# Windowed attention: the softmax sums applied after the value product instead of to the probabilities

## The chip, the cores and the metric

The kernel runs on one core of a Trainium2 chip. The metric is the time of one execution on the device in microseconds (us), given as the median of several runs. A core has five engines with an instruction queue each: TensorE (PE in the profile, with PEld for its weight loads), VectorE (DVE), ScalarE (ACT), GpSimd (POOL) and SyncE (SP, which here only starts DMA transfers). Each queue runs in order. An engine waits at an instruction until the semaphores that it names have been raised by the engines or transfers it depends on, and everything behind that instruction waits with it.

## The reference: what is computed

One layer of a hybrid encoder on 1024 tokens of width 1024, all in float32. Two mixers read the same normalised input: a windowed attention (8 heads of 64, two groups of keys and values, each query block of 128 tokens sees its own block and the two beside it) and a two-directional gated delta rule (4 heads of 128). Their outputs are multiplied with an output matrix and added to the input; a feed-forward part with squared ReLU and a last norm follow. The change touches the attention alone:

```python
scores = einsum("bnqkgd,bnskd->bnkgqs", qb, kb) * 64 ** -0.5
scores = scores + bias                                  # by head and distance
scores = where(valid, scores, -1e30)
probs = softmax(concatenate([scores, sink_col], -1), -1)[..., :-1]
out = einsum("bnkgqs,bnskd->bnqkgd", probs, vb)
```

The sink is one more logit of each head. It takes part in the maximum and in the sum, and has no value row.

## The kernel before

Tokens lie in 8 chunks of 128. The attention is a stream of 16 steps, one for each chunk `n` and key group `kv`; a step handles four heads, one for each `g`. In `attn_scores` the PE makes the scores of a head in one PSUM bank (a high and a low part of the keys, lines 542 and 543), and one DVE instruction (line 544) adds the bias, writes the scores to SBUF and keeps each row's maximum in `mx`. The DVE turns the four maxima into the negated maximum `nm` with the sink in it (line 551), and makes the sink's exponent `es` (line 552). The ACT takes the exponentials in place and keeps their row sums in `sm` (lines 553 and 556). The DVE adds the sink's part and inverts the sums (lines 557 and 558), and the four score tiles are multiplied with the inverse sums (line 561: three heads on DVE, the fourth on POOL). `attn_transpose` turns the normalised probabilities on the PE, one bank for each key block (line 571), and the ACT copies each bank to SBUF (line 573). After the second group of a chunk, `attn_value` multiplies them with the values: six float32 products of 512 columns for a chunk with three key blocks, four at the two ends (line 583), into one bank. Each row of that bank is a value channel and each column a query of a head, so a query's factor lies along the columns there. The DVE copies the bank out (line 586), and a transfer takes it to DRAM for the output projection.

The attention is one of two streams that `weave` merges by weights when the program is written. The other inverts triangular blocks (`invert`, lines 718 to 762) and then runs the delta rule in two directions (`scan`): 8 steps each way, in which small products (line 795) and DVE operations (lines 808 to 841) follow each other. Later in that stream `load_wout` brings in and splits the output matrix (ACT line 861, DVE and POOL line 863). After the attention, the output projection of the attention part (`out_attn`) and of the delta rule's part (`out_all`) run beside the rest of the scan. The program is written under a scheduler which reorders the instructions of each engine within their dependencies, so the order in which they stand is not that of the source alone; it is fixed when the kernel is built.

Tiles come from rings: `psA` and `psB` are four PSUM banks each, `pt` is a ring of 12 SBUF tiles, `nm` a ring of 12 small ones (128x4) for the maxima and sums of a step. The attention uses `psA` for scores, transposes and values; scan and inversion use `psB`.

Of the kernel before, what the change touches and what calls it, by code (L numbers as in the profile page):

```python
# [12 lines left out]
AF = mybir.ActivationFunctionType  # L13
ALU = mybir.AluOpType
AX = mybir.AxisListType

P = 128
# [60 lines left out]
class Block:  # L78
# [448 lines left out]
                self.nc.sync.dma_start(out=t[32 * m:32 * m + 32], in_=src)  # L527
            self.bias.append(t)

    def attn_scores(self, n, kv, mx, q, mk):  # L530
        nc = self.nc
        lo, hi = max(n - 1, 0), min(n + 2, NT)
        width, boff = (hi - lo) * P, (lo - (n - 1)) * P
        tiles = []
        for gp in range(2):
            s = mk((P, 2, 3 * P))
            for i in range(2):
                g = 2 * gp + i
                head = 4 * kv + g
                ps = self.ps("psA")  # L540
                keys = slice(lo * P, hi * P)
                nc.tensor.matmul(ps[:, :width], q[:, g, :], self.kh[kv][:, keys], start=True, stop=False)
                nc.tensor.matmul(ps[:, :width], q[:, g, :], self.kl[kv][:, keys], start=False, stop=True)
                nc.vector.tensor_tensor_reduce(out=s[:, i, :width], in0=ps[:, :width],
                                               in1=self.bias[head // 2][:, head % 2, boff:boff + width],
                                               op0=ALU.add, op1=ALU.max, scale=1.0, scalar=-3e38,
                                               accum_out=mx[:, g:g + 1])
            tiles.append(s)
        nm, es, sm = (self.small((P, 4), tag="nm", bufs=12) for _ in range(3))
        ns = self.nsink[:, 4 * kv:4 * kv + 4]  # L550
        nc.vector.scalar_tensor_tensor(out=nm, in0=mx, scalar=-1.0, in1=ns, op0=ALU.mult, op1=ALU.min)
        nc.vector.tensor_tensor(out=es, in0=nm, in1=ns, op=ALU.subtract)
        nc.scalar.activation(out=es, in_=es, func=AF.Exp)
        for g in range(4):
            s = tiles[g // 2][:, g % 2, :width]
            nc.scalar.activation(out=s, in_=s, func=AF.Exp, bias=nm[:, g:g + 1], accum_out=sm[:, g:g + 1])
        nc.vector.tensor_tensor(out=sm, in0=sm, in1=es, op=ALU.add)
        nc.vector.reciprocal(out=sm, in_=sm)
        for g in range(4):
            s = tiles[g // 2][:, g % 2, :width]  # L560
            (nc.gpsimd if g == 3 else nc.vector).tensor_scalar(out=s, in0=s, scalar1=sm[:, g:g + 1], scalar2=None,
                                                               op0=ALU.mult)
        return tiles, list(range(lo, hi))

    def attn_transpose(self, tiles, kbs):
        nc = self.nc
# [7 lines left out]
            out.append(pt)  # L574
        return out

    def attn_value(self, n, pts, kbs):
        nc = self.nc
        ps = self.ps("psA")
        last = len(kbs) - 1  # L580
        for j in range(last, -1, -1):
            for kv in (1, 0):
                nc.tensor.matmul(ps[64 * kv:64 * kv + 64, :], self.va[:, kbs[j], 64 * kv:64 * kv + 64],
                                 pts[kv][j].rearrange("p g q -> p (g q)"), start=j == last, stop=j == 0)
        o = self.pt()
        nc.vector.tensor_copy(out=o, in_=ps)
        nc.sync.dma_start(out=self.mad[n], in_=o)

    def query(self, n, kv):
# [5 lines left out]
    def attention(self):  # L595

        steps = [(n, kv) for n in range(NT) for kv in range(2)]
        qs = self.qs
        open_, pts = [], []

        def close():
            n, kv, tiles, kbs = open_.pop(0)
            pts.append(self.attn_transpose(tiles, kbs))
            yield 1.3
            if kv == 1:
                self.attn_value(n, pts[:], kbs)
                pts.clear()
                yield 2.6

        for i, (n, kv) in enumerate(steps):  # L610
            mk = self.pg if i % 3 == 2 else self.wr
            open_.append((n, kv, *self.attn_scores(n, kv, self.small((P, 4), tag="nm", bufs=12), qs.pop(0), mk)))
            if i + 2 < len(steps):
                qs.append(self.query(*steps[i + 2]))
            yield 1.3
            if len(open_) > 2:
                yield from close()
        while open_:
            yield from close()
# [758 lines left out]
```

## Time and profile before

| | |
|---|---|
| three runs | 1249.07, 1250.0 and 1251.16 us, median 1250.0 |
| the profiled execution | 1248.56 us, of which the span from first to last instruction is 1246.8 |
| PE busy | 1184.7 us, 95% of the span |
| DVE, ACT, POOL busy | 854.8, 620.7 and 577.9 us |
| first and last score product of the attention (line 543) | start at 333.4 and 447.3 us |
| last value product (line 583) | starts at 462.0 us |

The profile is one execution, seen by the hardware profiler. Its views are: the page with busy times and groups of instructions; the timeline, instructions in order of time; the waits, which say who waited for whom; and tables of busy time by stretch, in which PEclk is the clock that the PE was granted (1.00 is full). The records of PE products have modelled ends and overlap, so the time that one product costs in a row of products is read from the distance of their starts and not from the duration of a record. Names such as psA<-ident,wr stand for the tile that is written and, behind the arrow, for what is read. A float32 product appears as two PE records, a transpose as one.

### The profile page before, as it was taken

To read this page: it belongs to the slowest core of one execution; us is meant where nothing else is said; L and a number is where in the kernel's file an instruction comes from. 1 tells how busy PE (TensorE), PEld (TensorE's weight loads), DVE (VectorE), ACT (ScalarE), POOL (GpSimd) and SP (SyncE) were. 2 spreads that over 40 slices of the span, in tenths; PEclk is the share of its full clock that TensorE was granted. 3 is DMA by queue.
4 is the path that set the end of the run, shared out by engine and by line. 5 is a ranking of instruction groups with operands and counts; after the bars stand their busy time and mean duration, and the time that the engine had idled before them with its cause. 6 is when DMAs were issued, how large, how long until landed. Compare 5 with 4: busy or idle time off the path is not lost. (4 is left out here: it accounts for less than half of the span.)

```text
span 1246.8 us, 18527 instructions
## 1 busy us (share of the span) xinstructions
PE 1184.7 (95%) x6482; PEld 968.6 (78%) x6482; DVE 854.8 (69%) x1528; ACT 620.7 (50%) x1347; POOL 577.9 (46%) x488
## 2 busy tenths in 40 slices
PE   7999999899789989998899999999999999999997
PEld 5788877778568868877788888888777888888885
DVE  5677667982389986676645453544669797886976
ACT  6455688345485752125464554545545433444343
POOL 5354211352432333244564535535455555655595
PEclk9999999899889999999999999999999999999999
DMA  6134444341855668122234444443688624444333
GB/s 240 52 121 137 114 157 148 132 127 43 228 169 156 185 219 296 60 85 86 84 120 158 145 153 144 150 165 134 226 284 282 230 85 158 152 125 146 98 89 135
DMA packets 121630, 187.62 MB, mean 150 GB/s; under 512 B 11043, under 2 KB 64416, under 8 KB 121537
## 3 DMA queue, kind: packets, MB, share of 16 engines
q1 hardware_dynamic: 96708, 152.58, 37.6%
q10 hardware_dynamic: 16381, 29.67, 6.2%
q0 software_dynamic: 8448, 4.20, 1.8%
q8 instruction: 51, 0.84, 0.3%
q14 instruction: 42, 0.34, 0.1%
HBM read 122.39 MB, written 63.49 MB: 149 GB/s over the span
## 5 line engine op out<-in xcount | busy, mean ns | idle before, releaser
L124 PE MATMUL psA<-pg,wh 128*128 128x512 f32 x416 | 166.4, 401 | 2.1 <-ACT pt L456 2.1
L126 PE MATMUL psA<-pg,wl 128*128 128x512 f32 x416 | 165.7, 398 | 0.0
L125 PE MATMUL psA<-pg,wh 128*128 128x512 f32 x416 | 165.3, 397 | 0.0
L120 POOL TENSOR_TENSOR wl<-wr,wh 128x512 fp32r<-128x512 f32 x44 | 69.4, 1600 | 153.0 <-ACT wh L119 152.9
L1152 DVE TENSOR_TENSOR pg<-pg 128x512 fp32r<-128x512 f32 x112 | 123.1, 1133 | 19.5 <-ACT pg L1151 19.5
L120 POOL TENSOR_TENSOR wh<-wr,wh 128x512 fp32r<-128x512 f32 x32 | 47.7, 1511 | 129.1 <-ACT wh L119 129.1
L125 PE MATMUL psA<-pg,pg 128*128 128x512 f32 x256 | 99.8, 391 | 0.4 <-POOL pg L120 0.4
L124 PE MATMUL psA<-pg,pg 128*128 128x512 f32 x256 | 99.0, 391 | 1.1 <-DVE pg L1197 0.9
L126 PE MATMUL psA<-pg,pg 128*128 128x512 f32 x256 | 99.7, 389 | 0.0
L1069 ACT ACTIVATE pt<-pt 128x512 f32<-128x512 f32 x64 | 40.4, 631 | 117.6 <-DVE pt L1059 117.6
L120 POOL TENSOR_TENSOR pg<-wr,pg 128x512 fp32r<-128x512 f32 x48 | 73.4, 1558 | 50.8 <-ACT pg L119 50.8
L124 PEld LDWEIGHTS psA<-pg,wh 128*128 128x128 f32 x416 | 79.5, 191 | 19.9 <-ACT pt L456 2.4
L125 PEld LDWEIGHTS psA<-pg,wh 128*128 128x128 f32 x416 | 79.4, 191 | 18.4 <-issue 0.9
L126 PEld LDWEIGHTS psA<-pg,wl 128*128 128x128 f32 x416 | 79.4, 191 | 16.9
L1151 ACT CAST pg<-pg 128x512 fp32r<-128x512 f32 x112 | 66.8, 620 | 42.0 <-DMA pg<-sd 30.3
L125 PE MATMUL psB<-pg,pg 128*128 128x512 f32 x192 | 75.0, 391 | 0.8 <-POOL pg L120 0.7
L126 PE MATMUL psB<-pg,pg 128*128 128x512 f32 x192 | 75.0, 390 | 0.3 <-DVE pg L1152 0.3
L124 PE MATMUL psB<-pg,pg 128*128 128x512 f32 x192 | 74.7, 390 | 0.3 <-ACT pg L1151 0.3
L119 ACT CAST wh<-wr 128x512 fp32r<-128x512 f32 x76 | 43.6, 623 | 43.9 <-PE psA L125 24.3
L1059 DVE TENSOR_TENSOR pt<-psB,pt 128x512 f32<-128x512 f32 x39 | 26.9, 690 | 56.0 <-PE psB L126 29.9
L1059 DVE TENSOR_TENSOR pt<-psA,pt 128x512 f32<-128x512 f32 x39 | 26.8, 689 | 54.0 <-PE psA L126 38.8
L124 PEld LDWEIGHTS psA<-pg,pg 128*128 128x128 f32 x256 | 48.0, 188 | 12.7 <-DVE pg L1197 2.2
(385 smaller groups left out, 3303.7 us busy)
## 6 DMA issues: line engine op xcount, KB each, us to landing
sd<-pt ACTq DMA_DIRECT2D x112, 256.0 KB, 2.1
pg<-sd SPq DMA_DIRECT2D x112, 256.0 KB, 2.9
wr<-in_w_ffn_in SPq DMA_DIRECT2D x32, 512.0 KB, 3.7
wr<-in_w_in SPq DMA_DIRECT2D x22, 512.0 KB, 5.4
pg<-in_x SPq DMA_DIRECT2D x16, 512.0 KB, 4.9
wr<-in_w_ffn_out SPq DMA_DIRECT2D x16, 512.0 KB, 5.1
sc<-kvd SPq DMA_DIRECT2D x14, 512.0 KB, 6.4
kvd<-pt SPq DMA_DIRECT2D x16, 256.0 KB, 2.6
```

Of the source, the lines that this page charges most:

```text
L119: nc.scalar.copy(out=h, in_=raw)
L120: (eng or nc.gpsimd).tensor_tensor(out=l, in0=raw, in1=h.bitcast(F32), op=ALU.subtract)
L124: nc.tensor.matmul(ps, wh, xh, start=first, stop=False, skip_group_check=onto)
L125: nc.tensor.matmul(ps, wh, xl, start=False, stop=False, skip_group_check=onto)
L126: nc.tensor.matmul(ps, wl, xh, start=False, stop=last, skip_group_check=onto)
L1059: self.nc.vector.tensor_tensor(out=out, in0=in0, in1=in1, op=ALU.add)
L1069: self.nc.scalar.activation(out=c, in_=c, func=AF.Relu)
L1151: nc.scalar.copy(out=s[:, 0], in_=raw)
L1152: v.tensor_tensor(out=s[:, 1], in0=raw, in1=s[:, 0].bitcast(F32), op=ALU.subtract)
```

## The change

The probabilities stay unnormalised until the end. Line 544 gets another operation pair: the score plus bias is multiplied by -1, and the minimum of that is kept, with the negated sink as its start, so the accumulated value is the negated maximum itself and line 551 of before falls away. The exponentials get a scale of -1 to undo the sign. The sink's difference and the addition to the sums (lines 552 and 557 of before) move from DVE to POOL. The four multiplications of the score tiles fall away. In `attn_value`, eight small products spread the inverse sums: the weights are one column of inverse sums read 64 times with a step of zero, the moving operand is the 128x128 identity, and the result of head `g` and group `kv` is that head's inverse sums along the columns, the same in 64 rows. The ACT copies this bank to SBUF, and the copy-out of the values becomes a multiplication with it.

```diff
 attn_scores:
                 nc.vector.tensor_tensor_reduce(out=s[:, i, :width], in0=ps[:, :width],
                                                in1=self.bias[head // 2][:, head % 2, boff:boff + width],
-                                               op0=ALU.add, op1=ALU.max, scale=1.0, scalar=-3e38,
-                                               accum_out=mx[:, g:g + 1])
+                                               op0=ALU.add, op1=ALU.min, scale=-1.0, scalar=ns[:, g:g + 1],
+                                               accum_out=nm[:, g:g + 1])
...
-        nc.vector.scalar_tensor_tensor(out=nm, in0=mx, scalar=-1.0, in1=ns, op0=ALU.mult, op1=ALU.min)
-        nc.vector.tensor_tensor(out=es, in0=nm, in1=ns, op=ALU.subtract)
+        nc.gpsimd.tensor_tensor(out=es, in0=nm, in1=ns, op=ALU.subtract)
         nc.scalar.activation(out=es, in_=es, func=AF.Exp)
...
-            nc.scalar.activation(out=s, in_=s, func=AF.Exp, bias=nm[:, g:g + 1], accum_out=sm[:, g:g + 1])
-        nc.vector.tensor_tensor(out=sm, in0=sm, in1=es, op=ALU.add)
+            nc.scalar.activation(out=s, in_=s, func=AF.Exp, scale=-1.0, bias=nm[:, g:g + 1],
+                                 accum_out=sm[:, g:g + 1])
+        nc.gpsimd.tensor_tensor(out=sm, in0=sm, in1=es, op=ALU.add)
         nc.vector.reciprocal(out=sm, in_=sm)
-        for g in range(4):
-            s = tiles[g // 2][:, g % 2, :width]
-            (nc.gpsimd if g == 3 else nc.vector).tensor_scalar(out=s, in0=s, scalar1=sm[:, g:g + 1], scalar2=None,
-                                                               op0=ALU.mult)
-        return tiles, list(range(lo, hi))
+        return tiles, list(range(lo, hi)), sm
 attn_value(n, pts, kbs, rs):
+        inv, o = self.ps("psA", (P, 4, P)), self.pt()
+        for g in range(4):
+            for kv in range(2):
+                nc.tensor.matmul(inv[64 * kv:64 * kv + 64, g, :], rs[kv][:, g:g + 1].to_broadcast([P, 64]), self.ident,
+                                 start=True, stop=True)
+        nc.scalar.copy(out=o, in_=inv.rearrange("p g q -> p (g q)"))
         ps = self.ps("psA")
...
-        o = self.pt()
-        nc.vector.tensor_copy(out=o, in_=ps)
+        nc.vector.tensor_tensor(out=o, in0=ps, in1=o, op=ALU.mult)
         nc.sync.dma_start(out=self.mad[n], in_=o)
```

In the changed kernel the lines behind this place have numbers three higher: the score products are lines 544 and 545, the score sum 546, the sink's difference 551, the sum's addition 557, the inversion 558, the transposes 567, the copies of them 569, the spreading products 578, the copy of the spread sums 580, the value products 585, the multiplication 587; the scan's line 795 is 798, its lines 808 to 841 are 811 to 844, and line 863 is 866.

The first place is the PE's queue at the value products of one middle chunk. Before, `psA_4405` is the last bank of transposes, `psA_4440` the bank of the values, and the `psB` rows belong to the scan.

```order
L571 MATMUL psA_4405<-ident,wr_4138 128x128 x2
L571 MATMUL psA_4405<-ident,wr_4147 128x128 x2
L795 MATMUL psB_4412<-sc_4330,sc_4329 128x128 x2
L795 MATMUL psB_4417<-sc_4330,sc_4329 128x128 x2
L795 MATMUL psB_4422<-sc_4204,pg_4325 128x128 x2
L795 MATMUL psB_4427<-sc_4330,pt_4332 128x128 x2
L583 MATMUL psA_4440<-pt_4410,pg_2387 64x512
L583 MATMUL psA_4440<-pt_4322,pg_2387 64x512
L583 MATMUL psA_4440<-pt_4403,pg_2387 64x512
```

The same place in the changed kernel: `nm_4035` and `nm_4115` are the inverse sums of the chunk's two groups, `psA_4408` the bank into which they are spread, `psA_4419` the bank of the values.

```order
L567 MATMUL psA_4373<-ident,wr_4125 128x128 x2
L798 MATMUL psB_4399<-sc_4174,pg_4299 128x128 x2
L798 MATMUL psB_4404<-sc_4304,pt_4306 128x128 x2
L798 MATMUL psB_4441<-sc_4304,pg_4298 128x128 x2
L578 MATMUL psA_4408<-ident,nm_4035 64x128
L578 MATMUL psA_4408<-ident,nm_4115 64x128
...
L798 MATMUL psB_4446<-sc_4304,pg_4298 128x128 x2
L585 MATMUL psA_4419<-pt_4378,pg_2387 64x512
L585 MATMUL psA_4419<-pt_4296,pg_2387 64x512
```

The eight spreading products (two are shown) stand between the last transposes and the values, after the transposes of both groups.

The second place is the DVE's queue at the end of one step. Before, `nm_4158` holds the sums of the step whose exponentials lie in `wr_4138` and `wr_4147`; `nm_4266` belongs to the next step, and `pg_4025` is the scan's output.

```order
L558 RECIPROCAL nm_4158<-nm_4158 128x4
L841 TENSOR_TENSOR pg_4025<-pg_4025,psB_4253 128x256
L561 TENSOR_SCALAR wr_4138<-wr_4138,nm_4158 128x384 x2
L561 TENSOR_SCALAR wr_4147<-wr_4147,nm_4158 128x384
L544 ISA wr_4276,nm_4266<-psA_4281,pg_3177 128x384
L544 ISA nm_4266 128x1
L551 SCALAR_TENSOR_TENSOR nm_4285<-nm_4266,nsink 128x4
L841 TENSOR_TENSOR pg_4025<-pg_4025,psB_4262 128x256
```

The same step in the changed kernel has its sums in `nm_4115`; `sc_4174` and `pg_4007` are the scan's, `pt_4199` the output of the chunk before, whose values lie in `psA_4209`.

```order
L866 TENSOR_TENSOR wl_4167<-pg_4165,wh_4166 128x512
L558 RECIPROCAL nm_4115<-nm_4115 128x4
L826 SCALAR_TENSOR_TENSOR sc_4174<-sc_4009,egl,psB_4218 128x128 x2
L826 SCALAR_TENSOR_TENSOR sc_4174<-sc_4009,egl,psB_4223 128x128 x2
L844 TENSOR_TENSOR pg_4007<-pg_4007,psB_4233 128x256
L587 TENSOR_TENSOR pt_4199<-psA_4209,pt_4199 128x512
L546 ISA wr_4249,nm_4246<-psA_4250,pg_3172,nsink 128x384
```

The three multiplications between the inversion and the scan's operations are gone, and the scan's operations stand right behind the inversion.

The third place is POOL's queue in the same part. Before, the multiplications of the fourth head stand between the loads of the queries (line 592) and the split of the output matrix (line 863).

```order
L592 DMA pt_4301<-qad 128x4x128
L561 TENSOR_SCALAR wr_4147<-wr_4147,nm_4158 128x384
L592 DMA pt_4389<-qad 128x4x128
L561 TENSOR_SCALAR wr_4276<-wr_4276,nm_4287 128x384
L561 TENSOR_SCALAR pg_4364<-pg_4364,nm_4375 128x384
L592 DMA pt_4518<-qad 128x4x128
L863 TENSOR_TENSOR wl_4452<-pg_4450,wh_4451 128x512
```

In the changed kernel two small operations of each step stand there instead, the second of each (line 557) on the way to the inversion.

```order
L551 TENSOR_TENSOR nm_4114<-nm_4113,nsink 128x4
L593 DMA pt_4275<-qad 128x4x128
L557 TENSOR_TENSOR nm_4115<-nm_4115,nm_4114 128x4
L866 TENSOR_TENSOR wl_4167<-pg_4165,wh_4166 128x512
L551 TENSOR_TENSOR nm_4247<-nm_4246,nsink 128x4
L593 DMA pt_4357<-qad 128x4x128
L557 TENSOR_TENSOR nm_4248<-nm_4248,nm_4247 128x4
```

The large multiplications have left POOL's queue, and the softmax sums of a step now pass through it, behind loads of queries and pieces of the output matrix.

More of the change, by code (lines that the diff above doesn't have):

```diff
@@ L528, in bias_table, with attn_scores @@
             self.bias.append(t)
-    def attn_scores(self, n, kv, mx, q, mk):
+    def attn_scores(self, n, kv, q, mk):
         nc = self.nc
+        nm, es, sm = (self.small((P, 4), tag="nm", bufs=12) for _ in range(3))
+        ns = self.nsink[:, 4 * kv:4 * kv + 4]
         lo, hi = max(n - 1, 0), min(n + 2, NT)
@@ L545, in attn_scores @@
                                                in1=self.bias[head // 2][:, head % 2, boff:boff + width],
-                                               op0=ALU.add, op1=ALU.max, scale=1.0, scalar=-3e38,
-                                               accum_out=mx[:, g:g + 1])
+                                               op0=ALU.add, op1=ALU.min, scale=-1.0, scalar=ns[:, g:g + 1],
+                                               accum_out=nm[:, g:g + 1])
             tiles.append(s)
[L549 to L552, printed above, removed]
+        nc.gpsimd.tensor_tensor(out=es, in0=nm, in1=ns, op=ALU.subtract)
         nc.scalar.activation(out=es, in_=es, func=AF.Exp)
@@ L575, in attn_transpose, with attn_value @@
         return out
-    def attn_value(self, n, pts, kbs):
+    def attn_value(self, n, pts, kbs, rs):
         nc = self.nc
+        inv, o = self.ps("psA", (P, 4, P)), self.pt()
[4 more added lines that the diff above has]
+        nc.scalar.copy(out=o, in_=inv.rearrange("p g q -> p (g q)"))
         ps = self.ps("psA")
@@ L598, in attention @@
         qs = self.qs
-        open_, pts = [], []
+        open_, pts, rs = [], [], []
         def close():
-            n, kv, tiles, kbs = open_.pop(0)
+            n, kv, tiles, kbs, r = open_.pop(0)
             pts.append(self.attn_transpose(tiles, kbs))
+            rs.append(r)
             yield 1.3
             if kv == 1:
-                self.attn_value(n, pts[:], kbs)
+                self.attn_value(n, pts[:], kbs, rs[:])
                 pts.clear()
+                rs.clear()
                 yield 2.6
@@ L611, in attention @@
             mk = self.pg if i % 3 == 2 else self.wr
-            open_.append((n, kv, *self.attn_scores(n, kv, self.small((P, 4), tag="nm", bufs=12), qs.pop(0), mk)))
+            open_.append((n, kv, *self.attn_scores(n, kv, qs.pop(0), mk)))
             if i + 2 < len(steps):
```

## The prediction

> **What bounds the kernel now.** I read the page first: the PE is busy for 95% of the span, so whatever is added to it is added to the time unless it falls into its gaps.
>
> ```profile
> PE 1184.7 (95%) x6482; PEld 968.6 (78%) x6482; DVE 854.8 (69%) x1528; ACT 620.7 (50%) x1347; POOL 577.9 (46%) x488
> ```
>
> The share is a mean, and the change works between 333 and 463 us only. So next comes the table of busy time by stretch: start of the attention beside the inversion, its middle beside the scan, its end, and the last part of the scan.
>
> ```profile
> core 0: us, PE busy (x) PEld busy (x) DVE busy (x) ACT busy (x) POOL busy (x), PEclk, DMA share, GB/s
> 333.00:376.00 43.00, 33.56 (x568) 27.14 (x568) 34.72 (x112) 33.16 (x86) 17.34 (x21) 0.84 0.67 195
> 376.00:450.00 74.00, 72.14 (x536) 61.21 (x533) 69.48 (x245) 47.75 (x141) 22.37 (x20) 1.00 0.66 182
> 450.00:470.00 20.00, 16.04 (x104) 11.09 (x103) 17.08 (x44) 10.26 (x27) 8.06 (x6) 1.00 0.68 243
> 530.00:540.00 10.00, 7.13 (x47) 6.16 (x46) 10.00 (x23) 3.26 (x11) 6.72 (x5) 0.93 0.25 79
> ```
>
> In the middle, both PE (72.14 of 74) and DVE (69.48) are nearly full. The PE has 1.86 us of gaps there, 43 - 33.56 = 9.44 at the start and 20 - 16.04 = 3.96 at the end: 15.3 in all. However much DVE time the change frees, the attention can gain no more than these gaps. The waits of the PE between 330 and 470 us say who owns them (total, times, longest):
>
> ```profile
> PE psB L718 <- DMA pg<-atd: 3.4, 2, 1.7
> PE psB L751 <- DVE pt L744: 3.1, 2, 2.5
> PE psB L795 <- DVE sc L813: 2.7, 3, 1.2
> PE psA L571 <- DVE pt L586: 1.7, 1, 1.7
> PE psA L583 <- ACT pt L573: 1.6, 2, 0.9
> PE psB L795 <- DVE sc L808: 0.6, 1, 0.6
> PE psB L759 <- ACT pt L753: 0.5, 1, 0.5
> PE psB L795 <- DVE sc L823: 0.5, 1, 0.5
> PE psA L542 <- DVE pt L586: 0.4, 1, 0.4
> PE psA L542 <- DMA pt<-qad: 0.4, 1, 0.4
> ```
>
> DVE owns 3.1 + 2.7 + 1.7 + 0.6 + 0.5 + 0.4 = 9.0 us, ACT 1.6 + 0.5 = 2.1, transfers 3.4 + 0.4 = 3.8. The last stay. So 11.1 us can be won, and the question is what the PE pays for it.
>
> **Added on the PE: 64 spreading products.** Eight for each of eight chunks. They have float32 weights of 128x64 and 128 moving columns, which no row shows together. The value products have the same weights with 512 columns: 44 of them (six in six chunks, four in two) leave 88 records, so the new ones will leave 128. The timeline gives distances of starts:
>
> ```profile
> L583 PE MATMUL psA<-pt,pg x88: 592/592/644, 358.0 to 462.0; 128*64 128x512 f32 x88
> ...
> 384.77 0.33 PE L543 MATMUL psA<-pg,pt 128*128 128x384 f32 x1
> 384.94 1.05 PE L795 MATMUL psB<-sc,sc 128*128 128x128 f32 x8
> 385.83 0.61 PE L795 MATMUL psB<-sc,pg 128*128 128x128 f32 x4
> ...
> 391.71 2.80 PE L583 MATMUL psA<-pt,pg 128*64 128x512 f32 x12
> 394.44 0.44 PE L542 MATMUL psA<-pg,pt 128*128 128x384 f32 x1
> ...
> 355.97 0.22 PE L759 MATMUL psB<-wh,pt 64*64 64x64 f32 x1
> ...
> 356.79 0.22 PE L759 MATMUL psB<-wh,pt 64*64 64x64 f32 x1
> ```
>
> Eight L795 records take 385.83 - 384.94 = 0.89 us, 0.111 each. Twelve L583 records take 2.73 us, 0.228 each, so 128 columns of moving operand are a quarter of that, 0.057. The inversion's products with 64-column weights have 14 distances from the first to the last row shown (of the `wh` tile): 0.82 / 14 = 0.059, although only 64 columns move; it is their weights that take it, and a record of 128-column weights (0.111) takes twice that. With 64 columns of weights and 128 of moving operand both sides thus come to 0.057 to 0.059. I take 0.058: 128 x 0.058 = 7.4 us. The bounds are 0.057 (7.3 us) and the 0.111 of full weights (14.2 us). It is nearest to the first as long as weights load beside the stream ahead of them, and they do: the L543 record, with 128-column weights, takes 384.94 - 384.77 = 0.17 us, three quarters of 0.228 for three quarters of 512 columns. Below nothing it can't be, since no PE work is removed.
>
> The Trainium skill (TensorE: Matmul & The Clock Gate, "LDWEIGHTS (loading the stationary operand)") gives columns / 1.2 as the ns of a weight load, 53 for 64 and 107 for 128; the trace agrees with 0.059 and 0.111 us. The same page ("Back-to-back issue gap") speaks against the change: it has a sustained 81 ns for a product of 128 columns, from which I estimate 128 x 0.081 = 10.4 us, 3.0 above my term. It gives 131 ns for 512 columns, where this trace has 0.228 us, so I leave the sum to the rows.
>
> **Removed from DVE, moved to POOL and ACT.**
>
> ```profile
> L561 DVE TENSOR_SCALAR wr<-wr,nm 128x384 f32<-128x384 f32 (+1 forms) x33 | 16.6, 556 | 0.2
> L561 DVE TENSOR_SCALAR pg<-pg,nm 128x384 f32<-128x384 f32 (+1 forms) x15 | 7.9, 577 | 0.1
> L551 DVE SCALAR_TENSOR_TENSOR nm<-nm,nsink 128x4 f32<-128x4 f32 x16 | 4.3, 272 | 0.3
> L552 DVE TENSOR_TENSOR nm<-nm,nsink 128x4 f32<-128x4 f32 x16 | 2.7, 167 | 0.2
> L557 DVE TENSOR_TENSOR nm<-nm,nm 128x4 f32<-128x4 f32 x16 | 2.5, 156 | 2.1 <-ACT nm L553 1.5 <-ACT wr L556 0.4
> L586 DVE COPY pt<-psA 128x512 f32<-128x512 f32 x8 | 5.5, 684 | 1.6 <-PE psA L583 1.5
> L561 POOL TENSOR_SCALAR wr<-wr,nm 128x384 f32<-128x384 f32 (+1 forms) x11 | 14.1, 1284 | 49.3 <-DVE nm L558 26.3 <-DVE nm L552 9.6 <-ACT pt L753 6.9
> L561 POOL TENSOR_SCALAR pg<-pg,nm 128x384 f32<-128x384 f32 (+1 forms) x5 | 6.8, 1354 | 12.7 <-DVE nm L558 9.8 <-ACT pg L831 1.7 <-DVE nm L552 1.2
> ...
> L1059 DVE TENSOR_TENSOR pt<-psA,pt x39: 675/691/694, 641.1 to 919.2; 128x512 f32<-128x512 f32 x39
> L573 ACT COPY pt<-psA x44: 562/586/607, 350.7 to 460.1; 128x512 f32<-128x512 f32 x44
> L188 POOL TENSOR_SCALAR sm<-sm x24: 190/192/1286, 6.2 to 1241.7; 128x1 f32<-128x1 f32 x24
> L904 POOL TENSOR_TENSOR sm<-sm,half_exp x8: 1006/1007/1362, 470.8 to 583.6; 128x4 f32<-128x4 f32 x8
> ```
>
> DVE loses 16.6 + 7.9 + 4.3 + 2.7 + 2.5 = 34.0 us of work. The copy of the values becomes a multiplication of PSUM with SBUF, as line 1059 does it: 691 against 684 ns, nothing. The score sum with another operation pair isn't shown; I take no change, and even 0.1 us on each of its 64 instructions would lie within the 34.0. Likewise the exponentials' scale. POOL loses 14.1 + 6.8 = 20.9 us and gets 32 small operations; between the plain one (0.19) and the power (1.01) that is 6 to 32 us, and a subtraction or addition is like the plain one: 6. POOL is busy for less than a third of the middle. ACT gets eight copies like line 573, 8 x 0.586 = 4.7 us, covered by its 74 - 47.75 = 26 us of idle time in the middle alone. What is late next, should that cover fail, is the value multiplication on DVE, then the values' bank, then the PE's scores in it. The two transfers a chunk (line 587 of before, the loads of the queries) stay as they are.
>
> So on the path stands only what the freed DVE time gives back. In the timeline, the normalisation is what stands ahead of the late operations:
>
> ```profile
> 347.52 0.42 DVE L744 TENSOR_SCALAR pt<-psB 32x256 f32<-32x256 f32 x1
> 388.25 1.74 DVE L561 TENSOR_SCALAR wr<-wr,nm 128x384 f32<-128x384 f32 x3
> 389.91 1.11 DVE L808 SCALAR_TENSOR_TENSOR sc<-psB,negc,sc 128x128 f32<-128x128 f32 x4
> 450.12 1.29 DVE L561 TENSOR_SCALAR pg<-pg,nm 128x256 f32<-128x256 f32 x3
> ```
>
> The scan's line 808 begins as soon as three multiplications end; line 744 stood behind line 557, which waited up to 1.5 us for ACT with the whole queue behind it; line 813 is late by another group at 450. The longest waits for line 744 (2.5), two of at most 1.2 for line 813, and 0.6 for line 808 should go: 5.5 us. The bounds are 0 and 11.1. The wait for line 586 I leave, because at 457 us a split of the output matrix stands ahead of it and not a multiplication.
>
> **Sum.** 7.4 - 5.5 = +1.9 us on the profiled execution's 1248.56, 1250.5. The median of the runs is 1250.0, 1.4 above that execution, so the forecast is 1252 for the median. Its own range is 1249 to 1256: the recovered time may be 8 or 4 us, and the order of the scan beside it shifts by a few us either way. A measurement here can tell about 0.2%, 2.5 us, from no change.
>
> **Rivals.**
> - *DVE was the real brake (faster).* Where both engines are nearly full, freeing one may speed up the other beyond the waits named. For it: DVE at 69.48 of 74 us, and 10.00 of 10 at 530 to 540. Against it: the PE's gaps are all there is to win, and in the middle, where most spreading products land, they are 1.86 us. Price, if all DVE and ACT waits go: 7.4 - 11.1 = -3.7, so 1246. It decides from 7.4 us recovered, two thirds of what there is, and can be measured as faster from 9.9.
> - *The weights aren't hidden (slower).* The new products change weights at each one, and may follow each other like line 795, at 0.111: 14.2 - 5.5 = +8.7, so 1259. For it: line 795 moves as many columns, and its 0.111 is also the sum of 0.057 for 128 columns and as much for 128 of weights. Against it: 0.17 for line 543, where the weights vanish. With 64 columns of weights such a sum is 0.085 a record, 10.9 us, so 1255. The Trainium skill's 81 ns (the same section) would be close to that.
> - *A new wait in the chain of the sums (slower).* The sums now go ACT, POOL, DVE, PE, ACT, DVE, and POOL's part stands behind query loads and splits of the output matrix; a late sum holds the inversion on DVE with the scan's operations behind it, or the spreading products with all of the PE. The new bank also takes one more place in the ring `psA`. If each chunk waits for one ACT copy, that is 8 x 0.586 = 4.7: 1252 + 4.7, so 1257. Against it: in the PE's order the products stand after both groups' transposes, when the sums of the first are a step old.
> - *It doesn't matter (no change).* The products may fall into waits that exist, such as the 3.8 us for transfers and the 2.1 us for ACT, and the rest is given back: 1250.
>
> **How the numbers follow.** The forecast gets 0.50, the faster rival 0.19, unhidden weights 0.13, the new wait 0.11, no change 0.07. The forecast lies at the edge of what can be told: I give 0.21 of its 0.50 to slower, 0.25 to the same, 0.04 to faster. The faster rival gives 0.16 to faster and 0.03 to the same; unhidden weights 0.13 to slower; the new wait 0.08 and 0.03 to the same; no change 0.07 to the same. Together 0.20 faster, 0.38 same, 0.42 slower. The range reaches from the faster rival to the unhidden weights, 1246 to 1259.
>
> **What the profile after would show.** Right: 128 records of line 578 at starts 0.058 us apart, some 4 to 5 us more PE work in the middle with hardly a gap left; DVE 34 us less busy; PE waits for lines 744, 808 and 813 (now 747, 811, 816) mostly gone; the attention ending within 3 us of before. Wrong: starts about 0.11 apart; waits of the PE for line 558 or 580; POOL's small operations near 1 us; or an attention that ends several us earlier, which would say that the DVE held the PE by more than its recorded waits.

## The result, and the profile after

The changed kernel takes 1259.1 us (median of 4 runs, 1257.25 to 1260.45) beside 1249.53 for the kernel before on the same chip: a ratio of 1.0079 (95% interval 1.0064 to 1.0094), 9.6 us slower. The forecast was 1252 with a range from 1246 to 1259.

The top line of the page after: PE is 9 us busier than before, DVE 34.0 us less.

```profile
PE 1193.7 (95%) x6610; PEld 974.5 (77%) x6610; DVE 820.8 (65%) x1432; ACT 624.3 (50%) x1355; POOL 566.4 (45%) x504
```

The table by stretch, for the three stretches of the attention that the prediction quoted (busy time of PE, PEld, DVE, ACT and POOL, then the granted clock of the PE):

```profile
333.00:376.00 43.00, 36.77 (x596) 29.00 (x598) 23.28 (x74) 33.64 (x87) 12.92 (x27) 0.80 0.67 188
376.00:450.00 74.00, 73.41 (x570) 61.69 (x566) 53.83 (x184) 47.89 (x141) 13.27 (x28) 1.00 0.58 167
450.00:470.00 20.00, 18.58 (x148) 13.98 (x149) 13.60 (x37) 12.66 (x32) 7.07 (x7) 1.00 0.72 235
```

In the middle the PE has 0.6 us of gaps left (1.86 before) and DVE 20 (4.5 before). The waits of the PE there, 333 to 470 us:

```profile
PE psB L721 <- DMA pg<-atd: 3.1, 2, 2.1
PE psB L754 <- DVE pt L747: 2.2, 2, 1.3
PE psA L544 <- DMA pt<-qad: 0.9, 1, 0.9
PE psB L798 <- DVE sc L816: 0.9, 1, 0.9
PE psB L798 <- DMA pt<-pd: 0.9, 1, 0.9
PE psA L567 <- DVE nm L546: 0.2, 1, 0.2
```

DVE owns 2.2 + 0.9 + 0.2 = 3.3 us instead of 9.0, ACT nothing instead of 2.1. The spreading products: one row for all 128 records, and two rows of the timeline, one chunk's sixteen records and what comes next.

```profile
L578 PE MATMUL psA<-ident,nm x128: 272/273/359, 355.7 to 463.4; 128*64 128x128 f32 x128
...
386.76 1.09 PE L578 MATMUL psA<-ident,nm 128*64 128x128 f32 x16
387.78 0.71 PE L798 MATMUL psB<-sc,pg 128*128 128x128 f32 x4
```

Sixteen records take 387.78 - 386.76 = 1.02 us, 0.064 each, 8.2 us in all. So far this is roughly the picture that the prediction drew. Most of the loss lies elsewhere. Here is the timeline of the PE at 585 us before and at 590 us after: token transposes (line 207), the transposes of the last output chunk's norm (line 908, after: 911), then output products (lines 124 to 126).

```profile
585.37 0.66 PE L207 MATMUL psB<-ident,pg 128*128 128x128 f32 x4 [0.58 <-ACT pg L964]
586.13 0.66 PE L908 MATMUL psA<-ident,wr 128*128 128x128 f32 x4
586.54 0.47 PE L124 MATMUL psA<-pg,pt 128*128 128x512 f32 x1
```

```profile
590.17 0.66 PE L207 MATMUL psB<-ident,pg 128*128 128x128 f32 x4 [0.70 <-ACT pg L967]
595.16 1.11 PE L911 MATMUL psA<-ident,wr 128*128 128x128 f32 x4 [4.34 <-DVE wr L908]
595.93 0.78 PE L124 MATMUL psA<-pg,pt 128*128 128x512 f32 x1
596.50 0.63 PE L125 MATMUL psA<-pg,pt 128*128 128x512 f32 x1
```

After, the PE waits 4.34 us for a DVE operation of `out_gdn` (line 908), and its first products afterwards are slow (0.63 us instead of 0.39). At the last token transposes it is 590.17 - 585.37 = 4.8 us behind the kernel before, at the first output product 595.93 - 586.54 = 9.4, and at the tenth 599.11 - 588.69 = 10.4. DVE's timeline shows why. First before, then after:

```profile
582.01 0.17 DVE L900 TENSOR_TENSOR sm<-sm,sq 128x4 f32<-128x4 f32 x1 [0.75 <-ACT scr L898]
582.21 0.17 DVE L901 TENSOR_SCALAR sm<-sm 128x4 f32<-128x4 f32 x1
582.41 0.18 DVE L902 RECIPROCAL sm<-sm 128x4 f32<-128x4 f32 x1
582.59 0.75 DVE L213 SCALAR_TENSOR_TENSOR pg<-psB,cols,pg 128x512 fp32r<-128x512 f32 x1
583.26 0.15 DVE L903 TENSOR_TENSOR sm<-sm,sq 128x4 f32<-128x4 f32 x1
...
585.39 0.68 DVE L905 TENSOR_TENSOR wr<-pg,sm 128x512 f32<-128x512 f32 x1
```

```profile
588.67 0.16 DVE L903 TENSOR_TENSOR sm<-sm,sq 128x4 f32<-128x4 f32 x1
...
590.38 0.16 DVE L904 TENSOR_SCALAR sm<-sm 128x4 f32<-128x4 f32 x1
...
592.43 0.16 DVE L906 TENSOR_TENSOR sm<-sm,sq 128x4 f32<-128x4 f32 x1
...
594.42 0.69 DVE L908 TENSOR_TENSOR wr<-pg,sm 128x512 f32<-128x512 f32 x1
```

The norm of output chunk 0 is a chain of four small operations, a power on POOL, and a multiplication. Before, three of the four stand ahead of the first token operation (line 213), and the chain takes 585.39 - 582.01 = 3.4 us. After, eight token operations of 0.7 us each (lines 213, 971 and 951) stand between its links, and it takes 594.42 - 588.67 = 5.75 us, from a start that is later too. The text of these lines is the same in both kernels; the scheduler orders each queue anew, and has put them another way some 120 us behind the last changed instruction.

### The profile page after: what moved, and what is told of

The parts are those of the page before. It is cut to its first block, busy times and chain, and to the rows that moved or that the text cites. A ratio compares the mean times of both kernels' runs of the same rounds, so it can differ in the third digit from the quotient of the medians.

```text
span 1258.7 us, 18708 instructions
## 1 busy us (share of the span) xinstructions
PE 1193.7 (95%) x6610; PEld 974.5 (77%) x6610; DVE 820.8 (65%) x1432; ACT 624.3 (50%) x1355; POOL 566.4 (45%) x504
## 5 line engine op out<-in xcount | busy, mean ns | idle before, releaser
L1155 DVE TENSOR_TENSOR pg<-pg 128x512 fp32r<-128x512 f32 x112 | 121.8, 1120 | 25.9 <-ACT pg L1154 25.7
L120 POOL TENSOR_TENSOR wh<-wr,wh 128x512 fp32r<-128x512 f32 x32 | 47.7, 1510 | 127.7 <-ACT wh L119 127.7
```

The lines of the kernel that those rows point to most:

```text
L120: (eng or nc.gpsimd).tensor_tensor(out=l, in0=raw, in1=h.bitcast(F32), op=ALU.subtract)
L1155: v.tensor_tensor(out=s[:, 1], in0=raw, in1=s[:, 0].bitcast(F32), op=ALU.subtract)
```

## The experiments

**The order at the last output chunk.** The theory: the late norm costs the 5.5 us or so by which the changed kernel falls further behind from the token transposes to the tenth output product, and the attention itself does what was forecast. The rivals: the wait only moves, or the attention is what lost.

```diff
-            nc.scalar.activation(out=scr, in_=o[:, h, :], func=AF.Square, accum_out=so[:, h:h + 1])
+            sq = nc.scalar.activation(out=scr, in_=o[:, h, :], func=AF.Square, accum_out=so[:, h:h + 1])
...      # r, m, z: the reciprocal, the second multiplication and the one that writes zc
+        self.gdn_ins = [i.ins for i in (sq, r, m, z)]
...      # in tokens_second, for k = 0 to 3
+            with self.tc.issue_after(self.gdn_ins[0]):
                 nc.scalar.activation(out=b12, in_=ps, func=AF.Copy, scale=self.w_ffn[:, k:k + 1])
...
+            with self.tc.issue_after(self.gdn_ins[min(k, 2) + 1]):
                 self.split_rows(ps, self.w_ffn, 4 + k, self.X["B22"])
```

The edges set only the place in a queue and add no wait for data. The whole chain then stands a little earlier than in the kernel before: all four small operations are ahead of the first token operation. This order is not quite that of the kernel before, then, and no run has the kernel before with it. From the first token transpose to the first output product it takes 587.25 - 581.16 = 6.1 us, against 586.54 - 579.85 = 6.7 before: 0.6 us in the traces, little beside what follows.

> The changed kernel with one thing set by hand: the norm of the last output chunk (lines 901 to 908) is queued on ScalarE and VectorE ahead of the token operations, as it stood before the change. Theory A (5.5 of the 9.6 us were lost there, in a 4.34 us wait of line 911 for VectorE, some 120 us behind the changed code): 1259.1 - 5.5 = 1253.6 us, no wait over 1 us at line 911, attention as in the changed kernel. Rival B (the wait only moves to the next place, since the token operations are late then): 1258 to 1259 us. Rival C (the loss lies in the attention; what was read at 590 us is one execution's chance): 1259 us.

Measured: 1251.53 us against 1249.17, ratio 1.0018 (1.0000 to 1.0035). The wait is gone; the PE at the same place:

```profile
586.89 0.60 PE L912 MATMUL psA<-ident,wr 128*128 128x128 f32 x4
587.25 0.47 PE L124 MATMUL psA<-pg,pt 128*128 128x512 f32 x1
...
589.39 0.39 PE L124 MATMUL psA<-pg,pt 128*128 128x512 f32 x1
```

So of 1.0079, 0.0061 (7.6 us, with an uncertainty of some 3) was the order; the change itself costs 0.0018, 2.2 us. Theory A holds, and its 5.5 us lie within the uncertainty.

To see whether that is the order's price or one execution's, the changed kernel ran again, and `scores_only` (below) ran both with the order set and without.

> The changed kernel unchanged, for its time beside the others and for a second execution's trace. Theory A (the order at the last output chunk is the loss): 1.006 to 1.008 of the time before, line 911 waits 4 to 5 us for VectorE again, and the attention (first score product to last value product), 134.8 us long in the first trace against 131.4 in order_fixed with the same order in it, comes out near 131.4: those 3.4 us were one execution's. Rival B: the attention is 134 to 135 us again, so that part belongs to the change, through the order.

> scores_only without the order set by hand; the scheduler, left alone, puts the last chunk's norm behind the token operations here too, though there is neither a spreading product nor a missing normalisation. Theory A (the order costs some 5.5 us by itself, whatever the attention does): 1249.1 + 5.5 = 1254.6 us and the wait of 4 to 5 us at the last chunk's transposes. Rival B (the order costs only where the attention ends late): within 2 us of scores_only.

Measured: `change_again` 1259.24 us, ratio 1.0094 (1.0073 to 1.0115), a little over the 1.006 to 1.008 expected; `scores_only_late` 1254.34 us, 1.0047 (1.0031 to 1.0062), against 1.0003 for `scores_only`. Both wait again:

```profile
PE psA L911 <- DVE wr L908: 4.2, 1, 4.2
```

```profile
PE psA L910 <- DVE wr L907: 4.3, 1, 4.3
```

The first row is `change_again`, the second `scores_only_late`, which has no spreading product and keeps the normalisation. The order alone thus costs 0.0044 to 0.0076 of the time, 5.5 to 9.5 us, whatever the attention does (each difference is uncertain by some 3 us). The price goes beyond the wait. The PE in `change_again`, comparable with `order_fixed` because there both reach 577 us within 0.5 us of each other:

```profile
592.16 1.11 PE L911 MATMUL psA<-ident,wr 128*128 128x128 f32 x4 [4.20 <-DVE wr L908]
592.93 0.77 PE L124 MATMUL psA<-pg,pt 128*128 128x512 f32 x1
...
594.35 0.63 PE L124 MATMUL psA<-pg,pt 128*128 128x512 f32 x1
594.78 0.63 PE L125 MATMUL psA<-pg,pt 128*128 128x512 f32 x1
...
596.91 0.58 PE L124 MATMUL psA<-pg,pt 128*128 128x512 f32 x1
```

The transposes start 592.16 - 586.89 = 5.3 us later than in `order_fixed`, the tenth product (596.91 against 589.39) 7.5 us later: for over 4 us the products are 0.43 us apart instead of 0.23. The stretches of `change_again` after the wait show the granted clock (the number behind POOL's busy time):

```profile
588.00:592.00 4.00, 0.00 (x0) 0.00 (x0) 4.00 (x9) 2.62 (x5) 2.65 (x3) 0.81 0.00 0
592.00:596.00 4.00, 3.84 (x11) 3.22 (x12) 0.86 (x2) 0.62 (x1) 2.44 (x2) 0.50 0.14 32
596.00:600.00 4.00, 4.00 (x16) 3.19 (x15) 0.69 (x1) 0.00 (x0) 0.07 (x1) 0.84 0.72 229
```

Half the clock from 592 to 596. The spans of the two are 9.3 us apart (1257.5 and 1248.2); another 1.7 lie in a wait for POOL's line 120 after 900 us (1.9 us against 0.2), which `scores_only` has as well (2.0), so it is not tied to this order. The other half of Theory A is settled too: the attention, from the first start of line 544 to the last of line 585, was 134.8 us long in the first trace and is 465.0 - 333.7 = 131.3 in the second, with the same order; 3.5 us of the first trace were that execution's and not the change's (its granted clock from 333 to 376 us was 0.80, in the second 0.84; that this is the reason is not shown). Two executions of one kernel can thus differ by 3.5 us in this length, so a smaller difference between two traces below shows nothing by itself.

**Products and normalisation, two by two.** With the order set, the changed kernel without any division, with the old division, and with both.

```diff
 # no_division, against order_fixed
-        inv, o = self.ps("psA", (P, 4, P)), self.pt()
-        ...
-        nc.scalar.copy(out=o, in_=inv.rearrange("p g q -> p (g q)"))
...
-        nc.vector.tensor_tensor(out=o, in0=ps, in1=o, op=ALU.mult)
+        o = self.pt()
+        nc.vector.tensor_copy(out=o, in_=ps)
 # scores_only: the same, and at the end of attn_scores
+        for g in range(4):
+            s = tiles[g // 2][:, g % 2, :width]
+            (nc.gpsimd if g == 3 else nc.vector).tensor_scalar(out=s, in0=s, scalar1=sm[:, g:g + 1], scalar2=None, op0=ALU.mult)
 # both_divisions: order_fixed with that loop added
```

> The changed kernel with the order of order_fixed, without the division: no spreading products, no copy of them, the values only copied. It leaves the normalisation out altogether. Theory A (the 64 products cost the 8.3 us that their records take on TensorE): 8.3 us under order_fixed, 1245.3 us. Rival B (they partly fill waits that are there anyway): 2 to 4 us under it, 1250 us. Rival C (their weights are not hidden and the queue of banks suffers too): 13 us under it, 1240.5 us.

> The changed score part (negated maximum from the score sum, difference and sum on POOL), the old normalisation (three heads on VectorE, one on POOL), no spreading products; order as in order_fixed. VectorE is relieved of some 5 of the 34 us only. Theory A (the 6 us of recovered waits come from the normalisation's 24.5 us): 5 us over no_division, 1250.5 us, as before. Rival B (they come from the chain of small operations that this part shortens): 1245 to 1246 us, as no_division. Rival C (the new chain is longer, with two visits to POOL): over 1252 us.

> scores_only and the spreading products with their copy and multiplication on top: it divides twice, so VectorE has the old load and TensorE the new one; order as in order_fixed. Theory A (products cost their records, waits and products add up): scores_only + 8.3, 1258.8 us. Rival B (with VectorE loaded, the products fall into TensorE's waits): scores_only + 3, 1253.5 us. With the other three this makes a table of two by two: normalisation on VectorE or not, products or not.

Ratios to the kernel before (intervals of about 0.0015 to either side), and the length of the attention in one execution of each (128.8 us before):

| | no products | 64 products |
|---|---|---|
| normalisation on DVE and POOL | `scores_only` 1.0003; 129.0 us | `both_divisions` 1.0030; 131.7 us |
| no normalisation | `no_division` 0.9967; 126.4 us | `order_fixed` 1.0018; 131.4 us |

Read by rows, the products cost 0.0027 (3.4 us) where DVE is loaded and 0.0051 (6.4 us) where it is not; in the attention's length 2.7 and 5.0. Read by columns, taking the normalisation away gains 0.0036 (4.5 us) without the products and 0.0012 (1.5 us) with them. Each of these differences is uncertain by some 0.002 (2.6 us). So `both_divisions` goes with its Rival B (3 us over `scores_only`) and not with A's 8.3, and `scores_only` with its Theory A (5 us over `no_division`); for `no_division` the measured 6.4 lies between A's 8.3 and B's 2 to 4 and excludes neither. That the products cost less where DVE is loaded would fit products that partly fill the waits which a loaded DVE leaves, but it is not shown: the difference of the two (0.0024) is no larger than its uncertainty, and that of the attention's lengths (2.3 us) is smaller than what one kernel's executions differ by. `scores_only` equals the kernel before within 0.0014: the new score part by itself neither gains nor loses that can be told, with POOL in the chain of the sums.

**Twice the products.**

```diff
-                nc.tensor.matmul(inv[64 * kv:64 * kv + 64, g, :], rs[kv][:, g:g + 1].to_broadcast([P, 64]), self.ident,
-                                 start=True, stop=True)
+                for _ in range(2):
+                    nc.tensor.matmul(inv[64 * kv:64 * kv + 64, g, :], rs[kv][:, g:g + 1].to_broadcast([P, 64]), self.ident,
+                                     start=True, stop=True)
```

> order_fixed with each spreading product issued twice (128 instead of 64, the second writes the same values over the first). Theory A (the first 64 partly filled what was left of the waits, 6.4 of their 8.2 us showing; the next 64 find nothing to fill): 8.2 us over order_fixed, 1259.7 us; records still 0.064 us apart. Rival B (weights exposed or a bank held longer): 11 us or more over it, 1262.5 us. Rival C (there are still waits to fill): 4 us over it, 1255.5 us.

Measured: 1260.92 us, 1.0105 (1.0082 to 1.0127), over `order_fixed` 9.4 us by the medians and 0.0087 or 10.9 us by the ratios, uncertain by some 3.5; the attention is 139.7 us long, 8.3 more. In the middle the PE has nothing left to fill; behind it stands one row of 32 spreading records with what comes next:

```profile
376.00:450.00 74.00, 74.00 (x591) 62.51 (x587) 48.94 (x163) 42.39 (x124) 12.06 (x25) 1.00 0.53 149
...
371.44 2.02 PE L579 MATMUL psA<-ident,nm 128*64 128x128 f32 x32
373.39 0.82 PE L799 MATMUL psB<-sc,sc 128*128 128x128 f32 x5
```

The row takes 373.39 - 371.44 = 1.95 us, 0.93 more than a row of sixteen (1.02), so the records added to it are 0.93 / 16 = 0.058 apart, and each row costs about 0.09 us besides. That is the prediction's 0.058; 0.064 is a row of sixteen with these 0.09 in it. Other rows are broken up here by products of the scan and cost more for it. Summed over all rows of line 579, up to the next product each time, 256 records take 17.6 us, against 8.4 for the 128 of `order_fixed`. The second set thus costs its records in full (A), 9.2 us rather than 8.2 with the broken rows. The total by itself doesn't tell A from Rival B's 11 us, but the distance of 0.058 speaks against exposed weights. The PE's waits for the scan's line 812 (811 in `order_fixed`) are 3.7 us against 2.1.

**Division without the PE.** If the relief of DVE is worth 4 us and the products eat it, the sums could be spread by transfers. First with a transfer per step, 4 bytes per element:

```diff
+        nc.sync.dma_start(out=self.rd[n, kv].rearrange("g q -> q g"), in_=sm)      # end of attn_scores
...      # out_attn, after the load of mix
+            inv = self.wr((P, 4, P))
+            for kv in range(2):
+                self.nc.sync.dma_start(out=inv[64 * kv:64 * kv + 64], in_=self.rd[c, kv].unsqueeze(0).to_broadcast([64, 4, P]))
+            self.nc.vector.tensor_tensor(out=mix, in0=mix, in1=inv, op=ALU.mult)
```

> The division without TensorE: each step's 128x4 inverse sums go to memory, the output projection of the attention reads them back spread over 64 partitions beside the values, and VectorE multiplies the two there (8 of 128x512); no spreading products, the values are copied by ScalarE; order as in order_fixed. Theory A (what no_division gained was its missing products and normalisation, and 5.5 us on VectorE in the projection hide there): as no_division, 1245 us, faster than both kernels. Rival B (the small transfers, 4 bytes apiece, or SP's queue behind a wait for the sums delay the score loads): 1250 us or more. Rival C (VectorE's product lies on the projection's path): 1245 + 5.5 = 1250.5 us.

Here the ACT copies the values out, which DVE did before. Measured: 1312.28 us, 1.0521 (1.0495 to 1.0548). Rival B, and far worse than its 1250. SP's queue stands behind the transfer of the sums (line 559), and the PE waits for loads of the scan behind it:

```profile
SPq L559 <- DVE nm L558: 54.7, 11, 10.2
```

```profile
PE psB L794 <- DMA pt<-pd: 28.5, 6, 12.3
```

```profile
rd<-nm SPq DMA_DIRECT2D x16, 2.0 KB, 10.8
```

The last row is that of the sums' transfers: 2 KB each, a median of 10.8 us from issue to landing. Another 12.9 us the PE waits for the ACT's copy of the values (line 583). How the loss divides among these is not shown, since the waits follow from each other in part. So the sums were turned into rows on the PE (two transposes a chunk), sent once per chunk next to the values' transfer, and the multiplication was tried on DVE and on POOL.

```diff
-        nc.sync.dma_start(out=self.rd[n, kv].rearrange("g q -> q g"), in_=sm)
...      # attn_value
+        for kv in range(2):
+            nc.tensor.transpose(inv[0:4, 0, kv, :], rs[kv], self.ident)
+        nc.scalar.copy(out=r[0:4], in_=inv[0:4, 0])
+        nc.sync.dma_start(out=self.rd[n].rearrange("k g q -> g k q"), in_=r[0:4])
...      # out_attn, rows_spread_pool only
-            self.nc.vector.tensor_tensor(out=mix, in0=mix, in1=inv, op=ALU.mult)
+            self.nc.gpsimd.tensor_tensor(out=mix, in0=mix, in1=inv, op=ALU.mult)
```

> The division without spreading products and without 4-byte transfers: per chunk TensorE turns the two 128x4 tiles of inverse sums into 4 rows (2 transposes instead of 8 products), ScalarE copies them, one transfer of 512-byte rows takes them to memory next to the one of the values, and the attention's output projection reads them back over 64 partitions and multiplies on VectorE (8 of 128x512); order as in order_fixed. Theory A (dma_spread lost its 65 us to SP's queue, which waited 54.7 us for the 16 sums of single steps, and to the small packets; both are gone): no_division's 1245.1 plus the 16 transposes at about 0.06 to 0.11, 1 to 2 us, 1246 to 1247 us, faster than both kernels. Rival B (any division by memory is late: the reads stand on SP's queue ahead of the scan's loads): 1252 us or more. Rival C (VectorE's 5.5 us lie on the projection's path): 1251 us.

> rows_spread with the eight multiplications of the projection on POOL instead of VectorE. Theory A (rows_spread lost its 7.6 us over no_division on VectorE, where each product stands in front of the scan's operations and waits for its transfer, 12.8 us in all): most of it comes back, 1246 to 1248 us, faster than before, and line 810's and 815's 5.5 us of waits after 466 us fall to 2. Rival B (the transfers themselves are late, and POOL's 1.3 us product lies on the chain of the projection's operands): 1252 us or more.

Measured: `rows_spread` 1252.78 us, 1.0027 (1.0011 to 1.0043); `rows_spread_pool` 1251.16 us, 1.0018 (1.0005 to 1.0031). The attention is short in both (127.7 and 125.5 us), so what it gains is given back behind it. The multiplication's group in each, DVE first (its last part is the engine's idle time ahead of it):

```profile
L889 DVE TENSOR_TENSOR wr<-wr,wr 128x512 f32<-128x512 f32 x8 | 6.7, 836 | 12.8 <-DMA wr<-rd 8.6 <-POOL pt L120 4.2
```

```profile
L889 POOL TENSOR_TENSOR wr<-wr,wr 128x512 f32<-128x512 f32 x8 | 10.2, 1281 | 10.2 <-DMA wr<-rd 8.1 <-DVE sm L909 1.5 <-issue 0.7
```

Either engine stands still for 8 us in all until the read lands. On DVE the scan's operations stand behind it: after 466 us the PE waits 2.9 us for line 810 and 2.6 for line 815, on POOL only 2.2 for line 810. Yet the time fell by no more than 1.6 us by the medians, within the uncertainty, so Theory A for `rows_spread_pool` fell. The time of `rows_spread` is the 1252 or more of its Rival B, but that rival's cause isn't seen: the PE waits only 0.4 us for the scan's loads there. Rival C (1251) doesn't carry the whole loss, since most of it stays with the multiplication on POOL. Where the loss goes stays open.

**The load on DVE, moved instead of removed.** `scores_only` with heads 1 and 3 normalised on POOL instead of head 3 alone.

```diff
-            (nc.gpsimd if g == 3 else nc.vector).tensor_scalar(out=s, in0=s, ...
+            (nc.gpsimd if g % 2 else nc.vector).tensor_scalar(out=s, in0=s, ...
```

> scores_only with two of the four heads normalised on POOL instead of one: VectorE loses 16 products of 0.56 us (8.9 us), POOL gains 16 of 1.25 us (20 us); order as in order_fixed. Theory A (the waits that VectorE still owns in the attention shrink with its load: the whole normalisation, 24.5 us, was worth 4 us between scores_only and no_division): 1.5 us less than scores_only, 1247.6 us. Rival B (POOL's slow product ends the wait of the transposes now): 1250 us or more.

Measured: 1244.77 us, 0.9966 (0.9953 to 0.9979), 4.1 us faster than the kernel before, and as fast as no division at all (0.9967). Theory A has the direction right, but its 1.5 us under `scores_only` are 4.3 by the medians. POOL has the room, 32 multiplications of 1.2 us; one of them shows as a wait of the PE:

```profile
L561 POOL TENSOR_SCALAR wr<-wr,nm 128x384 f32<-128x384 f32 (+1 forms) x22 | 26.8, 1224 | 10.1 <-DVE nm L558 10.1
L561 POOL TENSOR_SCALAR pg<-pg,nm 128x384 f32<-128x384 f32 (+1 forms) x10 | 12.7, 1276 | 3.5 <-DVE nm L558 3.4
```

```profile
PE psB L753 <- POOL wr L561: 2.0, 1, 2.0
PE psB L753 <- DVE pt L746: 0.9, 1, 0.9
```

This is the version that beats both kernels, with the order at the last output chunk set by hand, which `scores_only` has as well; without it no run was made. It takes load from DVE and gives the PE nothing. That this is the whole cause is not shown: the PE's waits for DVE, ACT and POOL between 333 and 470 us sum to 8.1 us here and to 10.2 in `scores_only`, 2.1 of the 4.3. What the scheduler's order elsewhere adds or takes away stays open.

## Why the prediction was right and wrong, step by step

- **The step that failed** is a sentence in the sum: "the order of the scan beside it shifts by a few us either way", the only thing said on order, and meant for the attention's own stretch. All costs were drawn up between 333 and 463 us, as if the rest of the program stayed as it was, so a loss at another place was a term of nothing. The rest did not stay: the norm of the last output chunk moved behind token operations at 590 us and cost 5.5 to 9.5 us. The prediction held the two orders against each other in the attention only. Why the scheduler turns it over is not settled; that a smaller change does it too is shown by `scores_only_late`.
- **The sum without that** came out near: +1.9 us forecast, +2.2 (0 to 4.4) measured in `order_fixed`. In part that is luck: the products showed 1.0 us less than their term and the recovered waits 1.4 less, and the two misses nearly cancel.
- **The spreading products**, 7.4 us: the records take 8.2 to 8.4, of which 6.4 show (uncertain by some 2.6) where DVE is relieved, and the next 64 show all of theirs. Bounds, nearest row and the 0.058 within a row were right; what the term left out is the 0.09 us or so of each row. The rival of unhidden weights (0.085 to 0.111) falls, and with it the 81 ns of the Trainium skill (TensorE: Matmul & The Clock Gate, "Back-to-back issue gap"): here it is 64 ns a record, with the ends of the rows in it.
- **The recovered waits**, 5.5 us: 1249.2 x 0.0033 = 4.1 us with all of the division gone and no products (`no_division`). The waits of DVE and ACT fell by 11.1 - 3.3 = 7.8 us in the changed kernel's trace, and those for transfers rose by 1.1. Why not all of this shows in the time is not settled. Line 744's (now 747's) wait stayed at 2.2 of 3.1 us, against the 2.5 that were to go; of line 813's 2.7 us (now 816) 0.9 stayed, and line 808's 0.6 went. The sign of 4 to 5 us more PE work in the middle could not come: the gaps there were 1.86 us, and it got 73.41 - 72.14 = 1.27.
- **DVE 34.0 us less**: 34.0 in the first trace (854.8 to 820.8), 26.0 in `order_fixed` (828.8). The first match is partly chance. The score sum with another operation pair was taken as unchanged; on 128x384 it went from 550 to 614 ns, and all its rows together from 30.9 to 34.8 us, 3.9 more, inside the 6.4 that had been allowed. Operations that the change doesn't touch differ between executions by as much: the largest group of DVE (line 1155, in `order_fixed` 1158) took 121.8 us in the first trace and 125.3 in `order_fixed`. The score sum before, then after:

```profile
L544 DVE CUSTOM_DVE_ANT_0 wr<-psA,pg 128x384 f32<-128x384 f32 x32 | 16.6, 550 | 2.2 <-PE psA L543 2.1
```

```profile
L546 DVE CUSTOM_DVE_ANT_0 wr<-psA,pg,nsink 128x384 f32<-128x384 f32 x32 | 18.7, 614 | 4.8 <-PE psA L545 4.8
```

- **Rivals.** That DVE was the real brake is half true: some 4.1 us could be won (2.4 to 5.9), and the products cost more. A new wait in the chain of the sums reached DVE and not the PE: DVE waited 4.4 us for POOL's line 557 in the first trace, where before it waited 1.9 for the ACT, and no wait of the PE for line 558 or 580 is listed. "No change" is near what the change does in its own place; the rival that came closest to the time, unhidden weights at 1259, had it for the wrong reason.

## What to carry to other kernels

Where a scheduler orders the queues, an edit reaches places that it doesn't name: compare the order of the whole program before and after, and look first at chains of small operations that one engine shares with bulk work ahead of a PE wait. Test the edit with that place pinned, or the order's cost (here several times the edit's own) is taken for the edit's. And where two engines are nearly full and a third has room, as POOL had here, try the load on the third before paying for it with the PE.

## What the runs showed of the hardware

A wait costs more than its length. After 4.2 us without work the PE's granted clock was 0.50 for the next 4 us and its 512-column records 0.43 us apart instead of 0.23, which added 2.2 us to the delay of 5.3. The Trainium skill (TensorE: Matmul & The Clock Gate, "What's actually happening") has the array at half its clock after an idle window of about 3.4 us, until it has been busy for about as long again; `change_again` agrees on the half clock, but the slow time there was longer, 592.2 to 597.3 us; in the first trace of the changed kernel, after 4.34 us of waiting, it was shorter, 595.2 to 597.8 us. The wait of 3.7 us for line 203 shortly before is followed by a halved clock too (in `order_fixed` 0.50 from 581 to 585 us).

A product with 64 columns of float32 weights and 128 moving columns, each record with a weight load of its own, takes 0.058 us per record within a row (`products_twice`), no more than either side alone (0.057 to 0.059), and 0.064 in rows of sixteen with the ends of the rows in it. And transfers of 512 elements of 4 bytes each, 2 KB in all, took 10.8 us to land (the median of sixteen in `dma_spread`).
